# VectorE in program order at the ends of the feed-forwards and through the Fourier mixing, and x += in quarters

## The chip, the cores and the metric

The kernel runs on one core of one Trainium2 chip. The metric is the device time of one execution in microseconds (us). Engines are called as the profile calls them: PE (TensorE, matrix products), DVE (VectorE), ACT (ScalarE), POOL (GpSimd), SP (SyncE, which issues nearly all DMAs).

## The reference, cut to what matters

Two layers work on 256 tokens of 2048 features. Layer 0 mixes by windowed attention and a gated delta rule, layer 1 by a two-dimensional Fourier transform. Each mixing ends in a square projection, and each layer in a feed-forward:

```python
def fourier_mix(h):
    hg = h.astype(jnp.float32).reshape(b, l, FOURIER_GROUPS, FOURIER_GROUP_DIM)
    y = jnp.fft.fft2(hg, axes=(1, 3), norm='ortho').real
...
for layer in range(DEPTH):
    mx = split(silu_c @ w_ada[layer] + b_ada[layer], N_MOD)
    h_x = modulate(rms_norm(x, g_pre_mix[layer]), mx[0], mx[1])
    y_x = attention_deltanet_mixer(h_x, ...)  or  fourier_mix(h_x) @ w_fourier[o]
    x = x + mx[2] * rms_norm(y_x, g_post_mix[layer])
    f_x = swiglu(modulate(rms_norm(x, g_pre_ffn[layer]), mx[3], mx[4]), w_gate, w_up, w_down)
    x = x + mx[5] * rms_norm(f_x, g_post_ffn[layer])
```

So there are four places at which a product y is normalized, scaled and added to x: after w_out and after the feed-forward in layer 0, after w_four (the kernel's name for w_fourier) and after the feed-forward in layer 1. At the first three a norm of the new x follows at once, ahead of the next products.

## The kernel before, in words

**Products.** The 256 tokens are two tiles (t = 0, 1) of 128. A weight tile of 128 x 1024 (512 KB) comes by DMA into `raw` (4 buffers) or `araw` (2 buffers). Each half of it is split into two parts for a product of full precision: ACT writes the high part `whi` (L198), DVE the low part `wlo` (L204), or POOL does for a share of them (`pool_share`). Both have 4 buffers, so splits run two weight tiles ahead of PE. PE does three matmuls for each half and token tile: 12 for a weight tile and both token tiles.

**The four ends** are all `out_proj`. The output has four strips of 512 features. Strips 0 to 2 do both token tiles together. The last strip goes by token tile: all of t = 0, then all of t = 1, with some of the split weights kept (in ZT, T, A, KTOK, VTOK). Here POOL takes a quarter of the low parts. Behind each token tile comes `tail`: `evac_y` (in a feed-forward the sum of two halves, L1143; then ACT squares it, L1145, and DVE multiplies it by the row of gains, L1146), the reciprocal root (L322 to L327), x += in pieces of 1024, 512 and 512 columns (L1169), squares of the new x on ACT (L1172), the second reciprocal root (L1179 on), and a diagonal matrix `St` (L1181). `pre_norm` then makes pieces of the normed x: PE multiplies x by `St`, ACT and DVE scale and shift (L1222), ACT copies the high part, DVE subtracts the low part (L1225), through an `E2` tile. E2 has 3 buffers, of which the matrices of the Fourier transform hold two during the mixing. At the end of the kernel, instead of squares, each x += piece is followed by a DMA to the output.

**The Fourier mixing** calls `over_d` (a product over the features of a group) for 6 groups of t = 0 first, then, group by group, `over_d` of t = 1 and `over_l` (a product over tokens).

**Modulation weights.** `silu(c) @ w_ada` is 320 dot products on DVE (L275, 128 x 1024 each, called ada dots here), each with a 512 KB DMA into `araw`. `every(us)` sets the pace at which the program puts them between other work; `ada_until(m)` puts in all that remain up to modulation m. In `out_proj` that is called behind strip 2. Pieces of pending work (`fin_y`, `tail`) are generators: `add` queues one, each `yield d` puts the rest d us later on a modelled clock of PE, `step` resumes what is due, `drain` finishes it.

**Order.** Outside `in_order(True)` a scheduler sets the order of all engines. Inside, DVE keeps the order in which the program was written, and the scheduler orders the others. Before, `in_order(True)` is switched off ahead of the last strip of every `out_proj`. SP, like every engine, works through its list in order: a DMA into a buffer that is still in use holds up those behind it.

## Time and profile before

| | |
|---|---|
| median of 3 runs | 2500.32 us (2495.74 to 2503.1) |
| the profiled execution | 2498.01 us, its span 2496.2 us (1.8 us lie around it) |
| granted PE clock | 0.978 of full speed, mean over the span |
| PE busy | 2382.9 us, 95% of the span |
| DVE, ACT, POOL busy | 1791.7, 1284.7, 84.7 us |

PE's busy time also counts matmuls that ran at half clock, and a wait of PE is where another engine or a DMA was late. The profile is of one execution, so sums over its rows are to be held against 2498.01 us, and the other runs show how far one execution lies from the next.

### The profile page before, as it was taken

What the parts mean: (1) busy time and instruction counts of PE and PEld (TensorE: products, weight loads), DVE (VectorE), ACT (ScalarE), POOL (GpSimd) and SP (SyncE); (2) the same over time, 40 slices, a digit from 0 to 9 for tenths busy, and PEclk for the clock granted to TensorE, in tenths of its full rate; (3) what the DMA queues carried; (4) which work ended last, traced back from release to release, by engine and by line L of the source; (5) the groups of instructions that cost most, each with busy time, mean ns of one, the idle gap of its engine ahead of it and who ended that gap; (6) DMA issues with size and microseconds to landing.
All of it is one profiled execution on the core that took longest, in us unless ns stands there. A gap on an engine that the chain in (4) does not pass through costs nothing.

```text
span 2496.2 us, 39579 instructions
## 1 busy us (share of the span) xinstructions
PE 2382.9 (95%) x14536; PEld 1982.1 (79%) x14536; DVE 1791.7 (72%) x3379; ACT 1284.7 (51%) x2314; POOL 84.7 (3%) x106
## 2 busy tenths in 40 slices
PE   7999899988999999999999999799999999999997
PEld 6888688966778788888888887777888888888886
DVE  5889788877575787777777787878666666555566
ACT  5347345463755645444454545546554544445455
POOL 1000000000000100000000001002000000000001
PEclk8999999989999999999999999999999999999998
DMA  8885777668256589888888898586576777656665
GB/s 302 289 291 180 230 226 259 210 219 275 69 185 205 177 309 314 311 306 317 318 311 313 309 321 305 206 294 217 189 239 233 234 238 243 192 183 190 189 202 192
DMA packets 218483, 611.04 MB, mean 245 GB/s; under 512 B 68904, under 2 KB 69912, under 8 KB 217520
## 3 DMA queue, kind: packets, MB, share of 16 engines
q1 hardware_dynamic: 168016, 581.59, 68.4%
q10 hardware_dynamic: 46528, 15.21, 2.5%
q0 software_dynamic: 3744, 11.71, 1.4%
q8 instruction: 114, 1.87, 0.3%
q14 instruction: 81, 0.66, 0.1%
HBM read 595.03 MB, written 13.40 MB: 244 GB/s over the span
## 4 chain that ended last, share of the span: by engine, by line
PE 78%; DVE 8%; DMA 7%; ACT 3%; issue 3%; POOL 0%; ACTq 0%; DVEq 0%; POOLq 0%
PE acc L133 68%; PE sm L133 9%; DMA araw<-in_ada_d 3%; DVE wlo L204 2%; DVE araw L275 2%; DVE C L524 1%; DVE S L1169 1%; PE sm L1252 1%; DMA T<-dz 1%; DMA dy<-T 1%; DMA T<-dy 1%; ACT whi L198 1%; DMA araw<-in_w_dn 0%; DMA dz<-Zc 0%; DMA smallr<-in_smallr 0%
## 5 line engine op out<-in xcount | busy, mean ns | idle before, releaser
L198 ACT ACTIVATE whi<-raw 128x512 fp32r<-128x512 f32 (+1 forms) x1324 | 831.1, 630 | 895.7 <-DVE wlo L204 465.5
L204 DVE TENSOR_TENSOR wlo<-raw,whi 128x512 fp32r<-128x512 f32 (+1 forms) x1306 | 893.9, 692 | 482.9 <-ACT whi L198 480.3
L133 PE MATMUL acc<-whi,S 128*128 128x512 f32 x3312 | 1058.6, 397 | 6.6 <-ACT whi L198 5.4
L133 PEld LDWEIGHTS acc<-whi,S 128*128 128x128 f32 x3312 | 626.5, 189 | 142.8 <-ACT whi L198 5.8
L133 PE MATMUL acc<-wlo,S 128*128 128x512 f32 x1656 | 650.6, 393 | 2.0 <-DVE wlo L204 2.0
L275 DVE SCALAR_TENSOR_TENSOR araw<-araw,cb 128x1024 f32<-128x1024 f32 x320 | 389.1, 1218 | 33.8 <-DMA araw<-in_ada_d 33.1
L133 PEld LDWEIGHTS acc<-wlo,S 128*128 128x128 f32 x1656 | 313.6, 189 | 72.5 <-DVE wlo L204 3.4
L133 PE MATMUL acc<-S,whi 128*128 128x256 f32 x1152 | 221.3, 287 | 3.1 <-DVE C L524 3.0
L133 PEld LDWEIGHTS acc<-S,whi 128*128 128x128 f32 x1152 | 184.1, 192 | 4.0 <-issue 3.1
L133 PE MATMUL acc<-S,wlo 128*128 128x256 f32 x576 | 163.3, 284 | 2.0 <-DVE wlo L204 2.0
L133 PE MATMUL acc<-whi,ZT 128*128 128x512 f32 x384 | 122.0, 391 | 0.0
L133 PEld LDWEIGHTS acc<-S,wlo 128*128 128x128 f32 x576 | 110.8, 192 | 2.7 <-DVE wlo L204 2.6
L133 PE MATMUL acc<-whi,KCH 128*128 128x512 f32 x320 | 111.1, 404 | 1.1 <-ACT whi L198 1.1
L133 PE MATMUL acc<-whi,A 128*128 128x512 f32 x312 | 105.5, 393 | 0.0
L133 PE MATMUL acc<-whi,T 128*128 128x512 f32 x296 | 99.5, 392 | 0.0
L133 PE MATMUL acc<-wlo,KCH 128*128 128x512 f32 x192 | 78.7, 410 | 7.0 <-DVE wlo L204 6.8
L133 PEld LDWEIGHTS acc<-whi,ZT 128*128 128x128 f32 x384 | 72.2, 188 | 15.2
L133 PE MATMUL acc<-wlo,ZT 128*128 128x512 f32 x192 | 75.5, 393 | 0.2 <-POOL wlo L204 0.2
L133 PEld LDWEIGHTS acc<-whi,KCH 128*128 128x128 f32 x320 | 62.2, 195 | 15.1 <-ACT whi L198 1.5
L133 PE MATMUL acc<-wlo,T 128*128 128x512 f32 x176 | 68.9, 391 | 0.0
L133 PEld LDWEIGHTS acc<-whi,A 128*128 128x128 f32 x312 | 58.6, 188 | 11.9
L133 PEld LDWEIGHTS acc<-whi,T 128*128 128x128 f32 x296 | 55.6, 188 | 12.2
(442 smaller groups left out, 2638.0 us busy)
## 6 DMA issues: line engine op xcount, KB each, us to landing
raw<-in_w_gu SPq DMA_DIRECT2D x347, 512.0 KB, 4.3
araw<-in_ada_d SPq DMA_DIRECT2D x320, 512.0 KB, 4.8
raw<-in_w_dn SPq DMA_DIRECT2D x179, 512.0 KB, 4.6
raw<-in_w_att SPq DMA_DIRECT2D x40, 512.0 KB, 4.5
raw<-in_w_gdn SPq DMA_DIRECT2D x34, 512.0 KB, 4.6
raw<-in_w_out SPq DMA_DIRECT2D x30, 512.0 KB, 3.5
raw<-in_w_four SPq DMA_DIRECT2D x30, 512.0 KB, 4.3
ZT<-in_ada_s SPq DMA_DIRECT2D x24, 512.0 KB, 4.5
```

Source lines behind the costliest of these rows:

```text
L133: nc.tensor.matmul(out, l, r, start=start, stop=stop)
L198: S.activation(hi[:, :w], raw[:, c:c + w], AF.Copy)
L204: eng.tensor_sub(lo[:, :w], raw[:, c:c + w], hi[:, :w].bitcast(F32))
L275: V.scalar_tensor_tensor(out=junk, in0=w, scalar=1.0, in1=rows, op0=ALU.mult, op1=ALU.mult, accum_out=dst)
L524: V.scalar_tensor_tensor(out=ca[:, :, lo:hi], in0=pv[:, :, lo + o:hi + o], scalar=wconv[:, blk, j:j + 1], in1=ca[:, :, lo:hi], op0=ALU.mul ...
L1169: V.scalar_tensor_tensor(out=x[:, t, sl], in0=y[:, t, sl], scalar=r, in1=x[:, t, sl], op0=ALU.mult, op1=ALU.add)
L1252: nc.tensor.transpose(p[:, i * P:(i + 1) * P], hv[t][:, i * P:(i + 1) * P], ident)
```

## The change

1. `in_order(add_)` stands in `out_proj` where `in_order(False)` stood. `add_` is true for the two feed-forwards' second halves, so DVE keeps the program's order through their last strips and tails. After the first feed-forward that lasts through the norm and the whole Fourier mixing, up to the new `in_order(False)` ahead of w_four. At the ends of w_out and w_four the scheduler orders DVE as before.
2. x += goes in four quarters of 512 columns, with `yield TY` (0.7 us on the modelled clock) ahead of each; the wait of 2.5 us ahead of the second root is gone. Other work of the program falls between the quarters.
3. In the last strip of a feed-forward the sum goes to an E2 tile instead of in place.
4. The output goes by 2 DMAs for t = 0 and 3 for t = 1, in place of 3 and 3.
5. In the mixing `drain("tail1")` finishes the second token tile's x += before the loop over groups, ada dots come at a pace of 2.6 us from there on, pending work is resumed in `over_d` and `over_l`, and the first weights of w_four are fetched at group 7.

```diff
+F9RATE = 2.6
-YSQ = 2.5
+TY = 0.7
...
         if add_:
-            V.tensor_tensor(out=dst, in0=p, in1=dst, op=ALU.add)
-            src = dst
+            src = e2([P, 512]) if n == 3 else dst
+            V.tensor_tensor(out=src, in0=p, in1=dst, op=ALU.add)
...
-            sq = col(3)
-            for h, sl in enumerate((slice(0, 1024), slice(1024, 1536), slice(1536, 2048))):
+            yield TY
+            sq = col(4)
+            for h in range(4):
+                sl = slice(h * 512, h * 512 + 512)
                 V.scalar_tensor_tensor(out=x[:, t, sl], in0=y[:, t, sl], scalar=r, in1=x[:, t, sl],
                                        op0=ALU.mult, op1=ALU.add)
                 if emit is None:
                     S.activation(y[:, t, sl], x[:, t, sl], AF.Square, accum_out=sq[:, h:h + 1])
-                else:
-                    emit(t, sl)
+                elif t == 0 and h % 2:
+                    emit(t, slice(h * 512 - 512, h * 512 + 512))
+                elif t == 1 and h:
+                    emit(t, slice(0, 1024) if h == 1 else sl)
+                yield TY
             if emit is not None:
                 return
-            yield YSQ
...
         every(0)
         ada_until(mods)
-        in_order(False)
+        in_order(add_)
...
     for g in range(FAHEAD):
         over_d(g, 0)
+    drain("tail1")
+    every(F9RATE)
     for g in range(9):
...
+        if g == 7:
+            pool_share[0] = 0.0
+            while len(ahead) < 1 + AHEAD:
+                ahead.append(load_w1(*seq.pop(0)) if isinstance(seq[0], tuple) else load_w1(seq.pop(0)))
     every(FRATE)
-    pool_share[0] = 0.0
     ada_until(7)
+    in_order(False)
     rows = make_row(mc[:, 1, 2], gains[:, 1, 1])
```

Lines shift by 1 to 5: L204 becomes L205, L275 L276, L1143 L1145, L1146 L1147, L1169 L1172, L1181 L1186, L1222 L1227, L1225 L1230. How the orders move is shown at three places; the number at the end of a name tells one tile from another.

**The end of the second feed-forward.** DVE behind t = 0 of the last strip, first before (acc_23836 is the product of t = 0, the next row's `wlo` belong to weights of t = 1):

```order
L204 TENSOR_TENSOR wlo_24044<-raw_24041,whi_24043 128x512
L1146 TENSOR_TENSOR S_1240_8401<-S_1240_8401,OG_23132 128x512
L324 TENSOR_SCALAR col_24026<-ssy_23135,col_24024 128x1
L204 TENSOR_TENSOR wlo_24048<-raw_24041,whi_24047 128x512
L325 RECIPROCAL col_24025<-col_24025 128x1
L326 SCALAR_TENSOR_TENSOR col_24027<-col_24025,col_24026 128x1
L1162 TENSOR_REDUCE col_24159<-ssy_23135 128x1
L327 SCALAR_TENSOR_TENSOR col_24025<-col_24027,col_24025 128x1
L322 TENSOR_SCALAR col_24165<-col_24159 128x1
L204 TENSOR_TENSOR wlo_24060<-araw_24057,whi_24059 128x512
L1169 SCALAR_TENSOR_TENSOR S_1234_8386<-S_1240_8401,col_24025,S_1234_8386 128x1024
L1169 SCALAR_TENSOR_TENSOR S_1234_8386<-S_1240_8401,col_24025,S_1234_8386 128x512 x2
```

and now:

```order
L1145 TENSOR_TENSOR E_5054_24033<-acc_23855,S_1240_8401 128x512
L1147 TENSOR_TENSOR S_1240_8401<-E_5054_24033,OG_23149 128x512
L323 TENSOR_SCALAR col_24044<-col_24028 128x1
L325 TENSOR_SCALAR col_24046<-ssy_23152,col_24044 128x1
L326 RECIPROCAL col_24045<-col_24045 128x1
L327 SCALAR_TENSOR_TENSOR col_24047<-col_24045,col_24046 128x1
L328 SCALAR_TENSOR_TENSOR col_24045<-col_24047,col_24045 128x1
L205 TENSOR_TENSOR wlo_24057<-raw_24054,whi_24056 128x512
L205 TENSOR_TENSOR wlo_24061<-raw_24054,whi_24060 128x512
L1172 SCALAR_TENSOR_TENSOR S_1234_8386<-S_1240_8401,col_24045,S_1234_8386 128x512
L205 TENSOR_TENSOR wlo_24075<-araw_24072,whi_24074 128x512
L1172 SCALAR_TENSOR_TENSOR S_1234_8386<-S_1240_8401,col_24045,S_1234_8386 128x512
```

All three pieces of x += stood between two splits before. Now a split or two stands between every two quarters. The splits that stood between the small instructions of the root are behind them now.

**The start of the Fourier mixing.** DVE behind t = 1 of the first feed-forward's last strip, before (acc products end, pieces L1222 and L1225 of t = 0, ada dots L275):

```order
L1146 TENSOR_TENSOR S_1240_8401<-S_1240_8401,OG_15078 128x512
L324 TENSOR_SCALAR col_16329<-ssy_15081,col_16327 128x1
L325 RECIPROCAL col_16328<-col_16328 128x1
L1225 TENSOR_TENSOR S_3190_16210<-E_3195_16219,S_3189_16209 128x4x128
L326 SCALAR_TENSOR_TENSOR col_16330<-col_16328,col_16329 128x1
L275 SCALAR_TENSOR_TENSOR araw_16785,adaacc_15850<-araw_16785,cb 128x1024
L1222 TENSOR_SCALAR E_3197_16231<-sm_16226,psc_16207,mc 128x128 x2
L143 TENSOR_TENSOR ZT_16212<-sm_16213,ZT_16211 128x258
L143 TENSOR_TENSOR ZT_16212<-sm_16246,ZT_16211 128x258
L1225 TENSOR_TENSOR S_3190_16210<-E_3197_16231,S_3189_16209 128x4x128
L327 SCALAR_TENSOR_TENSOR col_16328<-col_16330,col_16328 128x1
L275 SCALAR_TENSOR_TENSOR araw_16832,adaacc_15850<-araw_16832,cb 128x1024
```

and now:

```order
L1145 TENSOR_TENSOR E_3201_16258<-acc_16036,S_1240_8401 128x512
L1147 TENSOR_TENSOR S_1240_8401<-E_3201_16258,OG_15082 128x512
L144 TENSOR_TENSOR ZT_16221<-sm_16257,ZT_16220 128x258
L1227 TENSOR_SCALAR E_3205_16277<-sm_16272,psc_16216,mc 128x128 x2
L1230 TENSOR_TENSOR S_3191_16219<-E_3205_16277,S_3190_16218 128x4x128
L323 TENSOR_SCALAR col_16284<-col_16247 128x1
L325 TENSOR_SCALAR col_16286<-ssy_15085,col_16284 128x1
L326 RECIPROCAL col_16285<-col_16285 128x1
L327 SCALAR_TENSOR_TENSOR col_16287<-col_16285,col_16286 128x1
L328 SCALAR_TENSOR_TENSOR col_16285<-col_16287,col_16285 128x1
L144 TENSOR_TENSOR ZT_16221<-sm_16271,ZT_16220 128x258
L1172 SCALAR_TENSOR_TENSOR S_1234_8386<-S_1240_8401,col_16285,S_1234_8386 128x512
```

The ada dots are gone from here (the first stands behind `St` of t = 1), the root follows on piece 3, and the quarters of x += stand one by one between the splits of the mixing (L144).

**The change from strip 2 to the last strip of w_four.** DVE before (ZT_17381 is the low part of the last strip's second weight tile, wlo_17396 of its third):

```order
L204 TENSOR_TENSOR wlo_17256<-raw_17249,whi_17255 128x512
L204 TENSOR_TENSOR ZT_17381<-araw_17379,ZT_17381 128x512
L204 TENSOR_TENSOR wlo_17277<-raw_17274,whi_17276 128x512
L204 TENSOR_TENSOR wlo_17281<-raw_17274,whi_17280 128x512
L204 TENSOR_TENSOR wlo_17396<-araw_17393,whi_17395 128x512
L204 TENSOR_TENSOR wlo_17400<-araw_17393,whi_17399 128x512
L204 TENSOR_TENSOR wlo_17415<-raw_17412,whi_17414 128x512
L1146 TENSOR_TENSOR S_1240_8401<-acc_17125,OG_16734 128x512
L1162 TENSOR_REDUCE col_17515<-ssy_16737 128x1
L322 TENSOR_SCALAR col_17529<-col_17515 128x1
```

and now (ZT_17394 belongs to the second weight tile, wlo_17409 to the third):

```order
L205 TENSOR_TENSOR wlo_17327<-raw_17320,whi_17326 128x512
L276 SCALAR_TENSOR_TENSOR araw_17380,adaacc_15854<-araw_17380,cb 128x1024
L276 SCALAR_TENSOR_TENSOR araw_17383,adaacc_15854<-araw_17383,cb 128x1024
L1147 TENSOR_TENSOR S_1240_8401<-acc_17171,OG_16790 128x512
L276 SCALAR_TENSOR_TENSOR araw_17386,adaacc_15854<-araw_17386,cb 128x1024
L1147 TENSOR_TENSOR S_1240_8401<-acc_17172,OG_16790 128x512
L290 TENSOR_REDUCE mc<-adaacc_15854 128x16
L1163 TENSOR_REDUCE col_17528<-ssy_16793 128x1
L291 TENSOR_TENSOR mc<-mc,bada 128x16
L323 TENSOR_SCALAR col_17542<-col_17528 128x1
L1208 SCALAR_TENSOR_TENSOR psc_17658<-mc,gains 128x16
L205 TENSOR_TENSOR ZT_17394<-araw_17392,ZT_17394 128x512
```

SP at the same place, now (araw_17392 and araw_17406 are the second and third weight tiles of the last strip):

```order
L287 DMA araw_17377<-in_ada_d 128x1024
L189 DMA raw_17425<-in_w_four 128x1024
L287 DMA araw_17380<-in_ada_d 128x1024
L189 DMA raw_17444<-in_w_four 128x1024
L287 DMA araw_17383<-in_ada_d 128x1024
L287 DMA araw_17386<-in_ada_d 128x1024
L189 DMA raw_17460<-in_w_four 128x1024
L189 DMA araw_17392<-in_w_four 128x1024
L189 DMA araw_17406<-in_w_four 128x1024
```

Before, the last ada dot stood some 20 rows ahead of this place, among the splits for strip 1. Now 11 of them are in the mixing in place of 20; they go on through strip 2, and the last five stand among the splits at its end; the loads of the last strip's second and third weight tiles take the two `araw` buffers behind the last two dots.

## Rows read from the trace of the kernel before

**Rows 1.** The page's section 1: busy us, share of the span and instructions of each engine.

```profile
PE 2382.9 (95%) x14536; PEld 1982.1 (79%) x14536; DVE 1791.7 (72%) x3379; ACT 1284.7 (51%) x2314; POOL 84.7 (3%) x106
```

**Rows 2.** Windows: stretches of the span, busy us and instructions of each engine.

```profile
core 0: us, PE busy (x) PEld busy (x) DVE busy (x) ACT busy (x) POOL busy (x), PEclk, DMA share, GB/s
806.00:842.00 36.00, 32.06 (x167) 26.08 (x166) 30.24 (x66) 27.10 (x61) 8.46 (x6) 1.00 0.48 158
1463.00:1515.00 52.00, 52.00 (x229) 42.26 (x228) 43.45 (x72) 25.92 (x44) 0.00 (x0) 1.00 0.92 329
...
1560.00:1582.00 22.00, 16.65 (x81) 13.44 (x79) 19.07 (x42) 17.24 (x36) 4.29 (x4) 0.92 0.72 253
1582.00:1602.00 20.00, 11.54 (x70) 10.27 (x71) 17.75 (x42) 10.43 (x26) 0.00 (x0) 0.83 0.46 157
...
1645.00:1702.00 57.00, 56.62 (x239) 46.02 (x240) 42.64 (x69) 29.36 (x52) 1.52 (x1) 0.97 0.81 287
1702.00:1756.00 54.00, 48.06 (x219) 37.42 (x218) 45.34 (x87) 39.97 (x86) 14.05 (x10) 0.94 0.64 213
2466.00:2496.20 30.20, 16.74 (x60) 12.45 (x58) 18.38 (x31) 11.50 (x21) 4.46 (x4) 0.77 0.37 138
```

**Rows 3.** Timeline of PE, five stretches; in brackets the wait ahead and its releaser.

```profile
1566.03 0.50 PE L133 MATMUL acc<-wlo,A 128*128 128x512 f32 x1 [3.11 <-DVE wlo L204]
...
1575.22 1.95 PE L133 MATMUL sm<-St,S 128*128 128x128 f32 x16
...
1594.31 3.78 PE L133 MATMUL sm<-St,S 128*128 128x128 f32 x16 [6.79 <-DVE St L1181]
...
1645.38 0.51 PE L133 MATMUL acc<-wlo,KCH 128*128 128x512 f32 x1 [2.70 <-DVE wlo L204]
...
1740.50 0.73 PE L133 MATMUL acc<-ZT,S 128*128 128x512 f32 x2 [1.69 <-ACT S L1224]
...
2476.43 0.79 PE L133 MATMUL acc<-wlo,KCH 128*128 128x512 f32 x1 [3.05 <-DVE wlo L204]
```

**Rows 4.** Timeline of DVE: four of the eight x += groups, and the last multiply.

```profile
1561.76 3.62 DVE L1169 SCALAR_TENSOR_TENSOR S<-S,col,S 128x1024 f32<-128x1024 f32 x3
...
1735.43 3.65 DVE L1169 SCALAR_TENSOR_TENSOR S<-S,col,S 128x1024 f32<-128x1024 f32 x3
...
2471.12 4.65 DVE L1169 SCALAR_TENSOR_TENSOR S<-S,col,S 128x1024 f32<-128x1024 f32 x3
...
2487.47 0.69 DVE L1146 TENSOR_TENSOR S<-S,OG 128x512 f32<-128x512 f32 x1 [0.79 <-ACT K L1145]
...
2488.85 2.61 DVE L1169 SCALAR_TENSOR_TENSOR S<-S,col,S 128x1024 f32<-128x1024 f32 x3
```

**Rows 5.** Timeline of POOL beside the first and the third of these groups.

```profile
1562.80 1.36 POOL L204 TENSOR_TENSOR wlo<-araw,whi 128x512 fp32r<-128x512 f32 x1 [2.45 <-DMA raw<-in_w_dn]
...
2471.00 1.36 POOL L204 TENSOR_TENSOR wlo<-araw,whi 128x512 fp32r<-128x512 f32 x1 [4.48 <-ACT whi L198]
2473.95 1.27 POOL L204 TENSOR_TENSOR wlo<-raw,whi 128x512 fp32r<-128x512 f32 x1 [1.59 <-ACT whi L198]
```

**Rows 6.** Timeline of DVE at the start of the Fourier mixing.

```profile
1576.27 0.68 DVE L1143 TENSOR_TENSOR S<-acc,S 128x512 f32<-128x512 f32 x1
...
1593.97 0.28 DVE L1181 TENSOR_SCALAR St<-ident,col 128x128 f32<-128x128 f32 x1
```

**Rows 7.** Timeline of DVE at the start of the w_four projection.

```profile
1643.49 1.23 DVE L275 SCALAR_TENSOR_TENSOR araw<-araw,cb 128x1024 f32<-128x1024 f32 x1 [4.43 <-DMA araw<-in_ada_d]
```

**Rows 8.** DMA issues between 1632 and 1702 us: KB each, median us to landing.

```profile
raw<-in_w_four SPq DMA_DIRECT2D x23, 512.0 KB, 4.3
araw<-in_ada_d SPq DMA_DIRECT2D x10, 512.0 KB, 5.1
```

**Rows 9.** Page, section 5: groups by line; busy us, mean ns of one, idle before.

```profile
L198 ACT ACTIVATE whi<-raw 128x512 fp32r<-128x512 f32 (+1 forms) x1324 | 831.1, 630 | 895.7 <-DVE wlo L204 465.5
...
L275 DVE SCALAR_TENSOR_TENSOR araw<-araw,cb 128x1024 f32<-128x1024 f32 x320 | 389.1, 1218 | 33.8 <-DMA araw<-in_ada_d 33.1
```

More of the change, by code (lines that the diff above doesn't have):

```diff
@@ L1172, in tail @@
                     S.activation(y[:, t, sl], x[:, t, sl], AF.Square, accum_out=sq[:, h:h + 1])
-                else:
-                    emit(t, sl)
+                elif t == 0 and h % 2:
[3 more added lines that the diff above has]
+                yield TY
             if emit is not None:
                 return
-            yield YSQ
             s1 = col(1)
-            V.tensor_reduce(out=s1, in_=sq[:, 0:2], op=ALU.add, axis=AX.X)
-            r = rstd_m2(s1, sq[:, 2:3], D)
+            V.tensor_reduce(out=s1, in_=sq[:, 0:3], op=ALU.add, axis=AX.X)
+            r = rstd_m2(s1, sq[:, 3:4], D)
             V.tensor_scalar(dg[:, t], ident, r, -0.5, ALU.mult, ALU.mult)
@@ L1375, in over_d @@
             src = hsl(2 * g + kc, t)
+            step()
             for x_, y_ in three:
@@ L1390, in over_l @@
                         i += 1
+                step()
         yh, yl = yt[g // 2]
@@ L1424, in trunk @@
     drain()
+    in_order(False)
 def consts():
```

## The prediction

> **What bounds the kernel now.** I read the page first, then windows, then PE's timeline wherever a window showed PE short of work. PE is busy for 2382.9 us, 95% of its span of 2496.2 [rows 1], so everything that engine order can give back lies in some 113 us of PE's idle time and in matmuls at half clock. The windows say where. In long products PE has no gap (52.00 of 52 us, 229 matmuls, so 0.227 us for one and 2.7 us for the 12 of a weight tile). It falls short at the places that this change touches: 32.06 of 36 at the end of w_out, 16.65 of 22 in the last strip of the first feed-forward, 11.54 of 20 at the start of the mixing, 48.06 of 54 at the end of w_four, 16.74 of 30.2 at the end of the kernel [rows 2].
>
> The timeline names what was late. In both feed-forwards' last strips PE waits once for a low part: 3.11 and 3.05 us [rows 3]. On DVE the x += group of t = 0 stands ahead of these low parts, for 3.62 and 4.65 us [rows 4]. At the mixing the wait is 6.79 us for `St` [rows 3], which DVE starts at 1593.97, 17.7 us after it took up the last product at 1576.27 [rows 6]. At w_four's start PE waits 2.70 us for a low part [rows 3], and DVE had just started an ada dot for which it had waited 4.43 us, until its DMA landed [rows 7]. The 1.69 us at 1740.50 come right after an x += group of 3.65 us [rows 3, 4].
>
> A wait costs more than itself, since PE then works at half clock for a while: 16 matmuls take 1.95 us at 1575.22, but 3.78 us after the wait for `St` [rows 3]. The windows with such waits have granted clocks of 0.92, 0.83 and 0.77, against 1.00 in the long products [rows 2]; the two levels are 2.4 and 1.2 GHz. I price the stretch behind a wait of about 3 us at 1.5 to 2.5 us.
>
> **The change, part by part.** Plus is time saved.
>
> (a) End of the first feed-forward. The split that PE waited for is now behind one quarter of x += and no longer behind the group. The same 2048 columns take 2.61 us in the last group [rows 4], so a quarter takes 0.65 to 0.75. But the small instructions of the root and the two 0.69 us instructions of `evac_y`, between which splits stood before, now come ahead of the splits in one run, with DVE waiting for ACT's square in it (0.79 us where the last one shows it [rows 4]). I count some 3 us in which no split is made, in place of 3.6 plus those small ones, and more evenly spread after that. Of 3.11 plus 1.5 I take +1.7; bounds 0 (the same wait in another place) and +4.6.
>
> (b) Start of the mixing. 4 ada dots stood in DVE's way to `St`, 1.22 us each [rows 9]; now none do, which alone is +4.9. Against it, program order puts the sum of t = 1 into the one free E2 buffer, behind piece 2 of t = 0 and ahead of piece 3, and the root behind piece 3, which waits for ACT twice. Then come four quarters, each between splits that wait for PE and ACT. Chained by hand with 0.7 us for each large instruction and 2.5 us for a piece through E2, the sum starts 7 us after the last product, the quarters 13, and `St` 20.5 to 22.5; it was 18.8 (1575.22 to 1593.97). I take 2 us later, -2; bounds -5 and +2. The ada dots inside the mixing cost nothing while PE has its products: 11 take 13 us of DVE, where 20 took 24.
>
> (c) Start of w_four. The dots come evenly now and fewer are in flight there, so the wait of 4.43 us for one dot's DMA should not return. 2.70 plus 1.6 at half clock was lost; I take +3, bounds 0 and +4.3.
>
> (d) The change from strip 2 to the last strip of w_four. This is the part that speaks against the change. 20 ada dots now lie behind the mixing in place of 11, and the last five stand at the end of strip 2. They go through two `araw` buffers, so each load starts when the dot before the last is done, and takes 5.1 us [rows 8]. By hand, from the start of strip 2: 12 us until the fifth weight tile's split frees DVE for dot 17374, done at 13.7; so dot 17380 has its data at 18.8; dot 17377 ends at 18.5, so dot 17383 has its data at 23.6 and is done at 24.9. Only then can SP issue araw_17392, the last strip's second weight tile: it lands 4.3 us later [rows 8], and 0.63 us of ACT [rows 9] makes it 29.9. PE needs it at 23.2 (8 weight tiles at 2.72 and half a one). Before, that load was issued some 25 us ahead and PE went through there without a wait: 56.62 of 57 us were busy from 1645 to 1702 [rows 2]. So 6.7 us of waiting and about 1.5 at half clock, less a little that the other engines catch up: -7.5. Bounds: 0, should the scheduler's order on DVE run further ahead of PE than I think and the dots be done in time, and -10.
>
> (e) End of w_four and the norm behind it. Pieces of t = 0 no longer stand behind 3.65 us of x += for t = 1, from which PE's wait of 1.69 us came and a slower stretch behind it (the window's granted clock is 0.94 [rows 2]). `St` of t = 1 comes behind three more splits. +2, bounds 0 and +5. At the end of w_out, of the same form, DVE's order hardly moves: +0.5, bounds 0 and +1.
>
> (f) End of the second feed-forward. As in (a), but the group took 4.65 us, and behind 3.05 us of waiting came 2.4 us of half clock. I take +4, bounds +1 and +5.6. Behind the last product the multiply no longer waits 0.79 us for ACT's square [rows 4], since the sum has a tile of its own; the root still waits for the square, so 0.5. Four quarters in place of three pieces cost 0.1; one DMA less is off the end. +4.4 in all.
>
> Sum: 1.7 - 2 + 3 - 7.5 + 2.5 + 4.4 = **+2.1 us**. The profiled execution (2498.01) would become 2495.9, the median (2500.32), which is 2.3 us higher, 2498.2. I forecast **2497 us**, no change that can be told: a measurement of this kernel shows about 0.3%, or 7.5 us.
>
> **A rule weighed.** The x += group of 3.62 us has one POOL split beside it, that of 4.65 has two [rows 4, 5], and the last one of 2.61 comes when POOL has no split left: one POOL split costs such a group 1.0 us. The Trainium skill, page "SBUF — State Buffer", section "Who interferes with whom", says that a DVE instruction with two inputs in SBUF and a GpSimd instruction that reads SBUF exclude each other for a whole instruction, whichever starts first. The trace agrees in kind, at 1.0 us for each, where the whole POOL instruction is 1.27 to 1.36 us [rows 5]. By that rule quarters that stand alone could each meet a POOL split, where a group met one or two. In rows of this case: 4 quarters with a POOL split each would lose 4 us in place of 1 or 2, at two feed-forward ends, so the sum would fall by 4 to 5 us, to -3. I hold that against (a) and (f): POOL makes only a quarter of the low parts there, and a POOL split that meets no x += meets a low part on DVE. I give it 1 in 10, inside the forecast's range.
>
> **Rivals.**
>
> *The dots are done in time.* If (d) does not happen, the rest stands: +9.6, 2488 to 2491 us. For it: the loads overlap, and DVE's dots in strips 0 and 1 ran without PE waiting before. Against it: two buffers and a landing of 5.1 us set a pace that no order changes, and SP stands still for the loads behind. 0.28.
>
> *`St` comes much later.* Slower: in program order a single late split holds up every quarter behind it. If `St` of t = 1 starts 27 us after the last product rather than 21, (b) is -8 with the half clock behind it, and the sum about -5; with (d) at its lower end, -8. 2503 to 2508 us. It decides from 25 us on. For it: PE already falls to 11.54 of 20 us here [rows 2], and each piece crosses PE, ACT and DVE. Against it: four ada dots have left. 0.15.
>
> *The change does little.* The waits for low parts return at the next split, since DVE has the same work in the same strip (18.38 us busy of the last 30.2 [rows 2]) and ACT's halves come no sooner: (a), (c) and (f) at a third, (d) halved. 2499 to 2502. 0.07.
>
> **How the numbers follow.** Forecast 0.5, rivals 0.28, 0.15, 0.07. The forecast's own range is 2492 to 2503. To leave out 2 in 10 the range takes in most of the first two rivals: 2487 to 2506. Faster by over 0.3% (below 2492.8): nearly all of the first rival and a little of the forecast, 0.30. Slower (above 2507.8): the second rival with (d) at its lower end, and some of the forecast where bounds meet, 0.15. Same: 0.55.
>
> **What would show it.** (a), (f): PE's waits for a low part in the last strips below 2 us, with no x += longer than 1.3 us on DVE. (b): `St` 20.5 to 22.5 us after the last product. (c): no wait of PE above 1 us in the first strip of w_four. (d): one wait of PE of 4 to 8 us behind the first weight tile of w_four's last strip, ended by ACT's high part of a tile in `araw`, whose DMA was issued late. The forecast is wrong if that wait is missing, or if a new one of over 3 us stands inside the mixing, where PE had none.

## The result and the profile after

The changed kernel takes 2511.32 us (median of 6 runs, 2508.89 to 2515.91), the kernel before 2497.44 us beside it (6 runs): ratio 1.0055, 95% interval 1.0039 to 1.0072. It is slower, by 14 us. The profiled execution took 2514.42 us, with a span of 2512.6; before it was 2498.01 and 2496.2.

Windows of the changed kernel, columns as in [rows 2]. The clock of its times is its own, so the same work stands some us later:

```profile
806.00:842.00 36.00, 33.24 (x174) 27.67 (x173) 31.92 (x71) 29.48 (x68) 9.55 (x6) 1.00 0.51 161
...
1560.00:1582.00 22.00, 17.16 (x83) 12.05 (x81) 16.08 (x32) 16.11 (x35) 5.78 (x4) 1.00 0.73 236
1582.00:1602.00 20.00, 10.02 (x48) 8.31 (x48) 12.27 (x34) 9.43 (x26) 0.00 (x0) 0.66 0.00 1
...
1645.00:1702.00 57.00, 52.12 (x216) 41.35 (x216) 40.32 (x67) 24.68 (x44) 0.00 (x0) 0.97 0.88 306
1702.00:1756.00 54.00, 45.40 (x193) 33.89 (x193) 43.44 (x84) 36.09 (x78) 12.12 (x10) 0.94 0.75 258
...
2466.00:2512.00 46.00, 32.20 (x130) 23.12 (x128) 33.56 (x53) 24.35 (x44) 11.10 (x8) 0.94 0.57 192
```

The stretch from 1582 to 1602 has fallen to 10.02 us of PE work with a granted clock of 0.66, and those from 1645 and 1702 have lost 4.5 and 2.7 us. PE's timeline names the waits:

```profile
1562.20 0.50 PE L134 MATMUL acc<-wlo,A 128*128 128x512 f32 x1 [1.05 <-DVE wlo L205]
...
1597.61 3.79 PE L134 MATMUL sm<-St,S 128*128 128x128 f32 x16 [6.42 <-DVE St L1186]
...
1652.83 0.61 PE L134 MATMUL acc<-wlo,KCH 128*128 128x512 f32 x1 [3.69 <-DVE wlo L205]
...
1710.00 0.40 PE L134 MATMUL acc<-ZT,A 128*128 128x512 f32 x1
1717.10 1.52 PE L134 MATMUL acc<-ZT,T 128*128 128x512 f32 x2 [6.71 <-ACT ZT L199]
...
2475.53 0.50 PE L134 MATMUL acc<-wlo,KCH 128*128 128x512 f32 x1 [1.69 <-DVE wlo L205]
...
2489.55 0.50 PE L134 MATMUL acc<-wlo,A 128*128 128x512 f32 x1 [1.03 <-DVE wlo L205]
```

Of the two single waits of 3.11 and 3.05 us [rows 3] pieces are left, the longest 1.05 us at the first end and 1.69 us at the second, below 2 us as forecast. But at the second end there are seven of them, 4.7 us in all. The wait for `St` is 6.42 us, hardly shorter than before (6.79). Two others are longer: 3.69 us in w_four's first strip (2.70 before), and 6.71 us behind the first weight tile of w_four's last strip, which was not there before.

To set stages side by side I read from the timelines when PE reaches nine places, and took the eight intervals between them. So the time up to the norm behind w_out drops out, which differed by up to 12 us between profiles. The change touches only its end, w_out's first x +=, and from the small matmul that spreads w_out's gains to that norm it is 77.5 us in both kernels. The places, before and after: first matmul with `St` behind w_out (819.19, 820.12); the small matmul that spreads the gains in the first feed-forward (1454.82, 1453.79); last product of its last strip (1574.98, 1575.58); first matmul with the second `St` of the mixing (1594.31, 1597.61); the small matmul behind the mixing (1631.19, 1634.87); first matmul of w_four's last strip (1702.19, 1708.84), of its third weight tile (1704.94, 1720.14); the small matmul in the second feed-forward (2367.60, 2384.17); end of the last product (2485.96, 2503.03). Each column is the interval up to a place, in us more (+) or less than before. A row is one profile of each kernel, and the last column is the sum. The columns of the feed-forwards begin where the gains are spread, so each holds all four strips of that projection; "its last strip" holds only the first two weight tiles of that strip:

```
               w_out  ffn 1   to St  mixing  w_four  its last  rest,   ffn 2    sum
               end    strip 3        rest    0 to 2  strip     norm    strip 3
after          -2.0   +1.6    +2.7   +0.4    +3.0    +8.6      +1.4    +0.5    +16.1
after_again    -1.9   +1.3    +2.4   +1.6    +0.2    +8.1      +0.6    +0.5    +12.7
no_araw        -2.0   +2.3    +2.7   +0.4    +2.6     0.0      +3.9    -0.1     +9.8
dots_pace      -1.1   +3.5    +2.7   +0.4    +1.7    +1.6      -0.2    +0.5     +8.9
dots_early     -1.9   +2.6    +5.2   +3.0     0.0     0.0      -0.4    +0.5     +9.0
dots_both      -2.0   +3.3    +4.9   +2.8    +2.2    +1.6      +1.7    +0.5    +15.0
no_dots        -1.9   +3.4    +2.7   +1.6    -4.6     0.0      -0.4    +0.5     +1.2
mix_free       -2.0   -1.2    +7.5   +1.2    +2.8     0.0      -0.2    +0.5     +8.6
strip_free     -2.0   -1.8    +3.1   +1.6    +1.6    +8.9      -0.3    -0.1    +11.1
inplace_1      -2.0   +1.6    +2.7   +0.4    +1.2    +8.3      +1.9    +0.5    +14.5
tail_first     -1.1   +4.1    -0.4 (both)    +0.9    +9.8      +2.5    +0.5    +16.2
old_tail        0.0   +2.1    +1.9   +1.7    +0.8    +7.9      -0.5    +2.4    +16.3
own_n2         -1.9   +1.3    +3.0   +1.7    +1.6    +8.2      +2.6    +0.4    +16.7
ffn1_free      -1.9   +2.9    +2.7   +1.6    +1.4    +7.7      +2.4    -3.0    +13.6
three_ends     -2.0   -0.2     0.0    0.0    -0.5     0.0      -0.4    -2.0     -5.0
```

Two profiles of the same kernel (after, after_again) agree within 0.8 us in six columns, but differ by 2.8 us in w_four's strips 0 to 2 and by 1.2 us in the rest of the mixing. The experiments whose edits lie elsewhere show a wider spread: +1.3 to +3.5 in the first feed-forward, -0.3 to +2.6 behind the first tiles of w_four's last strip. A column is worth no more than that; steady are `St` at +2.4 to +2.7 and the second feed-forward at -0.1 to +0.5. Behind the last product 9.6 us are left, 10.2 before. The same kernel a second time, beside three experiments:

> The changed kernel once more, unaltered, beside the next three on one chip. All theories: 2508 to 2512 us where before stands at 2497, ratio 1.004 to 1.007.

It measured 2506.25 us, ratio 1.0051 (1.0033 to 1.0069).

### The profile page after: what moved, and what is told of

It reads as the page before. It is cut to its first block, busy times and chain, and to the rows that moved or that the text cites. A ratio compares the mean times of both kernels' runs of the same rounds, so it can differ in the third digit from the quotient of the medians.

```text
span 2512.6 us, 39611 instructions
## 1 busy us (share of the span) xinstructions
PE 2387.6 (95%) x14536; PEld 1980.1 (79%) x14536; DVE 1792.7 (71%) x3387; ACT 1287.8 (51%) x2326; POOL 86.3 (3%) x106
## 4 chain that ended last, share of the span: by engine, by line
PE 74%; DVE 9%; DMA 9%; issue 5%; ACT 3%; ACTq 0%; SPq 0%; POOL 0%; DVEq 0%; POOLq 0%
PE acc L134 65%; PE sm L134 8%; DMA araw<-in_ada_d 4%; DVE wlo L205 2%; DVE araw L276 2%; DMA T<-dz 1%; PE sm L1257 1%; DMA dy<-T 1%; DMA OG<-in_ada_s 1%; DVE C L525 1%; ACT whi L199 1%; DMA T<-dy 1%; DVE S L1172 1%; DMA dz<-Zc 0%; DVE E L276 0%
## 5 line engine op out<-in xcount | busy, mean ns | idle before, releaser
L205 DVE TENSOR_TENSOR wlo<-raw,whi 128x512 fp32r<-128x512 f32 (+1 forms) x1306 | 895.4, 695 | 459.6 <-ACT whi L199 457.5
L276 DVE SCALAR_TENSOR_TENSOR araw<-araw,cb 128x1024 f32<-128x1024 f32 x320 | 389.9, 1220 | 50.4 <-DMA araw<-in_ada_d 50.0
```

The costliest lines, as they stand in the source:

```text
L205: eng.tensor_sub(lo[:, :w], raw[:, c:c + w], hi[:, :w].bitcast(F32))
L276: V.scalar_tensor_tensor(out=junk, in0=w, scalar=1.0, in1=rows, op0=ALU.mult, op1=ALU.mult, accum_out=dst)
```

## The longest wait: five dots, two buffers

The rows of the changed kernel at the change to w_four's last strip, on SP (DMA issues):

```profile
1706.17 2.08 SPq L287 DMA_DIRECT2D araw<-in_ada_d  x2
1708.35 0.37 SPq L189 DMA_DIRECT2D raw<-in_w_four  x1
1711.98 2.07 SPq L189 DMA_DIRECT2D araw<-in_w_four  x2
```

on DVE:

```profile
1704.92 1.22 DVE L276 SCALAR_TENSOR_TENSOR araw<-araw,cb 128x1024 f32<-128x1024 f32 x1
...
1706.66 1.22 DVE L276 SCALAR_TENSOR_TENSOR araw<-araw,cb 128x1024 f32<-128x1024 f32 x1
...
1710.72 1.22 DVE L276 SCALAR_TENSOR_TENSOR araw<-araw,cb 128x1024 f32<-128x1024 f32 x1 [2.83 <-DMA araw<-in_ada_d]
...
1712.48 1.21 DVE L276 SCALAR_TENSOR_TENSOR araw<-araw,cb 128x1024 f32<-128x1024 f32 x1
...
1717.08 0.69 DVE L205 TENSOR_TENSOR ZT<-araw,ZT 128x512 fp32r<-128x512 f32 x1 [2.26 <-ACT ZT L199]
```

and on ACT:

```profile
1716.41 1.15 ACT L199 ACTIVATE ZT<-araw 128x512 fp32r<-128x512 f32 x2 [6.69 <-DMA araw<-in_w_four]
```

The dot at 1710.72 had waited 2.83 us for its load, issued at 1706.17 as soon as the dot two ahead had ended. It ends at 1711.88, and 0.1 us later SP issues the last strip's second weight tile, into the buffer just freed. That lands 4.4 us later at 1716.41, where ACT had waited 6.69 us, and PE goes on at 1717.10. So buffer, load, dot and load again stand in a chain, as forecast. If this is the cause, other buffers or fewer dots behind strip 2 take the wait away. Rivals were DVE's own time for the dots, and a general shortage of DMA.

**Other buffers (no_araw).**

```diff
-        raw = T([P, 1024], "araw", 2) if pace[1] and not pace[0] and nload[0] % 5 > 2 else T([P, 1024], "raw", 4)
+        raw = T([P, 1024], "araw", 2) if pace[1] and not pace[0] and nload[0] % 5 > 2 and not inmix[0] else T([P, 1024], "raw", 4)
```

(`inmix` is true from the start of w_four to the second feed-forward.)

> The changed kernel, but the weight tiles of w_four's last strip never use the two buffers of the ada dots; they take the four raw buffers. Same number of dots in every stage. Theory: the wait of 6 to 7 us behind the first weight tile of that strip is the load of the second tile, which can't be issued before the dot in its buffer is done; with other buffers the load is issued in time, the wait is at most 1.5 us, and the time falls by 6 to 8 us against the changed kernel, ratio 0.998 to 1.002. Rival: DVE's own work on five dots and their late data hold up the splits in DVE's queue whatever the buffer; then PE still waits 3 us or more there.

PE's timeline at the second weight tile shows no wait:

```profile
1700.42 0.39 PE L134 MATMUL acc<-ZT,A 128*128 128x512 f32 x1
1700.65 0.62 PE L134 MATMUL acc<-ZT,T 128*128 128x512 f32 x2
```

The time is 2501.52 us, ratio 1.0040 (1.0023 to 1.0057). The wait is gone with all dots in place, so the theory stands and DVE's time for the dots was not it. But by the table's sum only 3 to 6 of the 8 us came back: with four buffers for all weight tiles of the strip PE waits more often later, five times for 0.2 to 1.0 us between 1703 and 1711 us. That column is +3.9, where the runs that leave it alone have -0.3 to +2.6. So the `araw` buffers probably had a use there.

**Fewer dots behind strip 2 (dots_pace).**

```diff
-FRATE = 5.0
+FRATE = 2.8
```

> The changed kernel with one number changed: in the w_four projection the program puts in an ada dot every 2.8 us of its modelled clock in place of 5.0, so that none remain to be put in together behind strip 2. DVE keeps about the same number of dots in the projection, but only two stand behind the last splits of strip 2 and not five. Theory: the wait of 6.7 us at the last strip comes from the loads of its second and third weight tiles, queued behind the last five dots; it falls below 2 us, and the time falls by 6 to 9 us against the changed kernel, ratio to before 0.999 to 1.003. Rival: DMA is short in the whole projection, because nine more loads lie there; then the wait only moves to other strips and the time stays within 3 us of the changed kernel.

The wait fell to 0.6 us, and the column from +8.6 to +1.6. The profile was 2500.4 us long, yet the runs say 2506.06 us, ratio 1.0053 (1.0034 to 1.0071), where the sum of the row would be 1.0036. The profiled execution was the fastest of its six, and the median is that of the changed kernel, as the rival said. The mechanism is shown by the profile, the gain is not shown by the runs.

**Dots ahead of `St` (dots_early).**

```diff
+    every(F9RATE)
     for g in range(FAHEAD):
         over_d(g, 0)
     drain("tail1")
-    every(F9RATE)
```

> The changed kernel with one line moved: the pace of 2.6 us for ada dots begins ahead of the pieces of the first token tile in the mixing and not behind them, so three more dots come ahead of St of the second tile, in program order on DVE. Theory: the 20 us without DMA shrink and three fewer dots are left to w_four, so the wait at its last strip is 3 to 4 us and not 6.7; St comes up to 2 us later; the time falls by 2 to 5 us against the changed kernel. Rival: DVE's order ahead of St is so tight that each dot delays St by its whole 1.3 us and PE goes on at half clock longer; then the time stays the same or grows.

Three dots moved, and the whole 8.6 us of the last strip went, and the 3 us ahead of it too. But `St` came 2.5 us later than in the changed kernel, most of the 3.7 us that three dots take, and the rest of the mixing lost 1.4 to 2.6 us more. 2503.92 us, ratio 1.0043 (1.0028 to 1.0058). Both expectations were half right.

**Both (dots_both).** The two edits above together.

> The changed kernel with both changes to the dots' pace: it begins ahead of the first norm pieces, and in w_four it is 2.8 us. So no dot is left to be put in behind strip 2. Theory: the wait at w_four's last strip is gone (below 1 us), and what remains of the loss against before is the first feed-forward's end (1.5 us), the mixing's start (2.5 to 5 us) and the second feed-forward's end (0.5 us), less 2 us won at w_out: ratio 1.001 to 1.003. Rival: the dots' loads then compete with the weights in all strips and the loss in strips 0 to 2 grows to 4 us or more; ratio above 1.004.

2513.52 us, ratio 1.0077 (1.0060 to 1.0094): the worst. The last strip did lose its wait, but `St` waits longest of all, as PE shows:

```profile
1602.70 3.57 PE L134 MATMUL sm<-St,S 128*128 128x128 f32 x15 [9.08 <-DVE St L1186]
```

and w_four's strips lose 2.2 us again, with more dots in them. So theory and rival were both too simple: more dots cost ahead of `St`, and they cost in w_four. The stretch behind `St` was not tried: from 1602 to 1632 us PE of the changed kernel is busy for 29.29 of 30 us with nine dots in it, DVE for 22.57, and no experiment changed the pace there.

**No dots in w_four (no_dots).** From the seventh row of that modulation on the loads and dots are skipped and the sums set to zero:

```diff
-                        raw = T([P, 1024], "araw", 2)
-                        nc.sync.dma_start(raw, a["ada_d"][n, h])
-                        ada_dot(raw, cb[:, h], ac[:, k, h:h + 1], raw)
+                        if 134 <= n < 144:
+                            if n == 134 and h == 0:
+                                V.memset(ac[:, 6:], 0.0)
+                        else:
+                            raw = T([P, 1024], "araw", 2)
+                            nc.sync.dma_start(raw, a["ada_d"][n, h])
+                            ada_dot(raw, cb[:, h], ac[:, k, h:h + 1], raw)
```

> The changed kernel without the last 20 of the 32 ada dots of one modulation (their part of the sum is left out, set to zero), that is without any dot or dot's load in the w_four projection. The 11 dots in the mixing stay. Theory: dots in w_four cost 3 us in strips 0 to 2 (a wait for a dot's load) and 8 us at the last strip; without them both go, and the time is 9 to 12 us below the changed kernel, ratio to before 0.999 to 1.002, with 4 to 5 us of loss left at the first feed-forward's end and the start of the mixing, less 2 us won at w_out. Rival: w_four's first wait comes of the weights' own loads or of the row that is spread over the partitions there, not of the dots; then a wait of 2 to 3 us stays in strip 0.

2494.69 us, ratio 0.9999 (0.9985 to 1.0012), the table's two w_four columns at -4.6 and 0.0, and no wait of PE in w_four's strips 0 to 2. So the waits there hung on dots, by the same place also the 2.70 us of before with its half clock [rows 3]: by these two columns dots cost 4.6 us in the kernel before and 13 to 16 in the changed one. The rival falls.

Why are there more of them there? In the changed kernel no dot can run ahead of the second tile's `St`, since DVE's program order puts the first behind it. The loads of two dots fill their buffers, and SP stands at the third. DMA between 1580 and 1602 us (busy tenths and GB/s in 40 slices of 0.55 us), and SP's row:

```profile
DMA  0000000100000000000000000000000000000000
GB/s 22 0 0 0 0 0 0 30 0 0 0 0 0 0 0 0 0 0 0 0 0 0 0 0 0 0 0 0 0 0 0 0 0 0 0 0 0 0 0 0
```

```profile
1575.74 58.21 SPq L287 DMA_DIRECT2D araw<-in_ada_d  x11
```

11 issues take from 1575.74 to 1633.95; the first is at 1575.74, the second only at 1607.38, behind the first dot. Before, DMA moved 157 GB/s from 1582 to 1602 [rows 2]; now almost nothing moves for 20 us. The nine dots that w_four takes over are 4.7 MB of loads, 19 us at the mean rate of the kernel's page (243 GB/s).

## The first feed-forward's end and the mixing

DVE of the changed kernel at the start of the mixing:

```profile
1577.43 0.73 DVE L1227 TENSOR_SCALAR E<-sm,psc,mc 128x128 f32<-128x128 f32 x2 [1.64 <-ACT E L1225]
1578.92 0.69 DVE L1230 TENSOR_TENSOR S<-E,S 128x512 fp32r<-128x512 f32 x1 [0.76 <-ACT S L1229]
1580.55 0.73 DVE L1227 TENSOR_SCALAR E<-sm,psc,mc 128x128 f32<-128x128 f32 x2 [0.94 <-ACT E L1225]
...
1583.05 0.68 DVE L1145 TENSOR_TENSOR E<-acc,S 128x512 f32<-128x512 f32 x1
...
1585.58 0.73 DVE L1227 TENSOR_SCALAR E<-sm,psc,mc 128x128 f32<-128x128 f32 x2 [0.78 <-ACT E L1225]
...
1588.53 0.16 DVE L326 RECIPROCAL col<-col 128x1 f32<-128x1 f32 x1 [0.46 <-ACT col L324]
...
1597.27 0.29 DVE L1186 TENSOR_SCALAR St<-ident,col 128x128 f32<-128x128 f32 x1
```

DVE is not busy here: 12.27 of 20 us in the window. PE's waits for pieces ahead of `St` are seven with 5.2 us in all; before they were three with 3.2 us. A piece takes 3.1 us (1577.43 to 1580.55), with 0.76 to 1.64 us of waiting for ACT between its steps; the sum of the second tile (L1145), ready from 1576, comes at 1583.05 behind piece 2; the root at 1588.53 behind piece 3; `St` at 1597.27, 21.7 us after PE's last product.

**In the scheduler's order (mix_free).**

```diff
-        in_order(add_)
+        in_order(add_ and emit is not None)
```

> The changed kernel, but DVE's order in the first feed-forward's last strip and through the Fourier mixing is the scheduler's, as before (program order only at the end of the second feed-forward). Theory: the loss comes from program order in the mixing, which keeps the ada dots behind St of the second token tile, lets DMA stand still for 20 us and leaves 9 more dots to the w_four projection. Then the dots are back in the mixing, the wait of 6.7 us at w_four's last strip and the one of 3.7 us in its first strip go, and the time is 2495 to 2500 us, ratio to before 0.998 to 1.001. Rival: the quarters and the sum in an E2 tile cost as much by themselves, whatever the order; then it stays above 2505 us, ratio above 1.003.

2499.77 us, ratio 1.0031 (1.0016 to 1.0046): the ratio lies just above the rival's bound, the time is in the theory's range. The wait at w_four's last strip went, as the theory has it, and the feed-forward won 1.2 us over before. A wait of 3.89 us in w_four's first strip stayed, against the theory. Here DMA did not stand still (174 GB/s from 1582 to 1602 us), and between 1632 and 1702 us only 8 dots' loads were issued, where before had 10 [rows 8] and the changed kernel 18. So that wait needs dots, as no_dots shows, but neither the standstill nor more of them. And `St` came still later, which no theory had:

```profile
1597.62 3.78 PE L134 MATMUL sm<-St,S 128*128 128x128 f32 x16 [5.93 <-DVE St L1186]
...
1651.88 0.79 PE L134 MATMUL acc<-wlo,KCH 128*128 128x512 f32 x1 [3.89 <-DVE wlo L205]
```

`St` is used 26.9 us after the last product (1570.75). Quarters, the pace of the dots and the late `drain` lose 7.5 us here in the scheduler's order, more than in program order (2.7). So program order is a help at this place, and the rest of the edit delays `St` where the scheduler has the order. Which part of it does so no run tells apart.

**Program order from the mixing on (strip_free).** As mix_free, and `in_order(True)` ahead of the mixing's first `over_d`.

> The changed kernel, but the first feed-forward's last strip is in the scheduler's order, and program order begins behind it, at the first norm piece of the mixing. Theory: program order loses 1.5 us in that last strip, because DVE waits for ScalarE's squares and root with splits queued behind; that comes back, and the rest of the loss (mixing, w_four) stays: 1 to 3 us below the changed kernel, its last product 1.5 us earlier in the profile. Rival: that loss comes of the quarters in that strip; then the last product comes no earlier.

The last product came 3.4 us earlier by the table (-1.8 in place of +1.6; the profiles in program order have +1.3 to +3.5, and mix_free, in the scheduler's order there too, -1.2). So program order is what loses in that strip; the quarters by themselves win there. 2506.12 us, ratio 1.0043 (1.0030 to 1.0056).

**The sum in place (inplace_1).**

```diff
-            src = e2([P, 512]) if n == 3 else dst
+            src = e2([P, 512]) if n == 3 and own[0] else dst
```

(`own` is true in the second feed-forward.)

> The changed kernel, but the sum of the first feed-forward's last strip is made in place, as before, and not in an E2 tile; the second feed-forward keeps its E2 tile. Theory: at the start of the mixing only one E2 buffer is free, each norm piece holds it for 3.1 us, and the sum of the second token tile takes a turn in that line. Without it St of the second tile comes 2 to 3 us earlier after the last product, and the time falls by 2 to 4 us against the changed kernel. Rival: the line is DVE's program order and not the buffer, and in place the multiply waits 0.79 us for the square; then St comes no earlier and the time stays.

Nothing: `St` at +2.7 as in the changed kernel, 2506.42 us, ratio 1.0051 (1.0032 to 1.0070). My theory of the single E2 buffer falls; the multiply then waits for the square (0.87 us) in place of it.

**The tail first (tail_first).**

```diff
+    drain("tail1")
     for g in range(FAHEAD):
         over_d(g, 0)
-    drain("tail1")
```

> The changed kernel with one line moved: the x += of the second token tile is finished ahead of the first norm pieces of the mixing, in program order, and not behind them. Theory: St of the second tile is late because program order puts the sum behind piece 2, the root behind piece 3 and the quarters around piece 4, and each piece takes 3.1 us through ScalarE and VectorE in turn. With the tail first St comes about 10 us after the last product and not 21, the first pieces come 7 to 8 us later, and the wait for St goes; the start of the mixing gains 1 to 3 us in all. Rival: PE has nothing else to do ahead of the first piece, so the wait only moves there and half clock follows it; then the mixing ends later than in the changed kernel.

The wait for `St` is gone, and PE waits for the first pieces:

```profile
1582.09 3.03 PE L134 MATMUL sm<-C,S 128*128 128x258 f32 x12 [7.92 <-ACT S L1229]
...
1594.92 0.76 PE L134 MATMUL sm<-C,S 128*128 128x258 f32 x4 [2.32 <-ACT S L1229]
```

From the last product to the end of the mixing it is 55.8 us against 59.3 and 60.2 in the two profiles of the changed kernel and 56.2 before. But that last product came 2.4 us later, in a column that other runs move by up to 1.9 us without an edit there, and the runs show no gain: 2505.99 us, ratio 1.0051 (1.0035 to 1.0067). What decides the start of the mixing, other than that pieces and tail pass through ACT and DVE in turn, stays open.

## The ends of the feed-forwards

DVE of the changed kernel at the end of the second feed-forward, and ACT in its root:

```profile
2469.50 1.18 DVE L1147 TENSOR_TENSOR S<-S,OG 128x512 f32<-128x512 f32 x1 [0.79 <-ACT K L1146]
...
2484.18 0.69 DVE L1145 TENSOR_TENSOR E<-acc,S 128x512 f32<-128x512 f32 x1 [0.38 <-PE acc L134]
2484.90 0.69 DVE L1147 TENSOR_TENSOR S<-E,OG 128x512 f32<-128x512 f32 x1
...
2486.14 0.21 DVE L325 TENSOR_SCALAR col<-ssy,col 128x1 f32<-128x1 f32 x1 [0.48 <-ACT K L1146]
2488.27 0.16 DVE L326 RECIPROCAL col<-col 128x1 f32<-128x1 f32 x1 [1.92 <-ACT col L324]
...
2488.80 2.38 DVE L205 TENSOR_TENSOR wlo<-raw,whi 128x512 fp32r<-128x512 f32 x2
2491.11 0.74 DVE L1172 SCALAR_TENSOR_TENSOR S<-S,col,S 128x512 f32<-128x512 f32 x1
...
2495.51 1.77 DVE L1172 SCALAR_TENSOR_TENSOR S<-S,col,S 128x512 f32<-128x512 f32 x1
```

```profile
2486.65 1.28 ACT L324 ACT_TABLE_LOAD   x1
```

From 2483.66 to 2488.80 DVE makes no split. 0.48 and 1.92 us of it are waits for ACT, which makes a split of its own and then loads a table for the root (1.28 us). Before, three splits stood in these gaps. At the first feed-forward's end the stretch without a split is 4.4 us (1557.06 to 1561.45), with the same wait of 1.92 us. Ahead of that, each multiply of strip 2 waits 0.79 us for ACT's square with splits behind it: program order now covers that too, but own_n2 below shows that it costs nothing that the table can tell.

**The second feed-forward in the scheduler's order (ffn1_free).**

```diff
-        in_order(add_)
+        in_order(add_ and emit is None)
```

> The changed kernel, but DVE's order at the end of the second feed-forward is the scheduler's, as before. Theory: program order at that end gives and takes alike (PE waited 3.05 us and ran at half clock before, now it waits 4.7 us in seven pieces), so the time stays within 2 us of the changed kernel, ratio to before 1.004 to 1.006. Rival: program order there costs by itself, since DVE waits for ScalarE's squares and for its root with splits queued behind, and quarters in the scheduler's order would be better than both; then it gains 4 us or more against the changed kernel, ratio below 1.004.

The table's column of that end goes from +0.5 to -3.0, 3.5 us, nearly what the rival called for. The runs (2508.35 us, ratio 1.0058, 1.0040 to 1.0076) show nothing of it: by the ratio set ahead the theory stands. I take the rival as borne out by the profile alone, since that column is steady, and three_ends repeats it below.

**Strip 2 with a tile of its own (own_n2).** `n >= 2` in place of `n == 3` in `evac_y`.

> The changed kernel, but strip 2 of the feed-forwards also makes its sum in an E2 tile. In program order the multiplies of strip 2 wait 0.79 us each for ScalarE's square, with splits behind them, and PE waits 1.7 us for a low part right after it. Theory: that wait falls below 1 us at both feed-forwards' ends, and each gains 0.5 to 1.5 us; the time falls by 1 to 3 us against the changed kernel, too little to be told by the runs, but seen in the two profiles. Rival: what holds the splits there is the length of DVE's queue; then the wait of 1.7 us stays.

The multiplies no longer wait, but DVE's next split then waits 1.50 us for ACT's high part, and PE's wait went only from 1.69 to 1.53 us at the second end. The column did not move (+0.4), 2510.38 us, ratio 1.0071 (1.0056 to 1.0086). The theory falls.

**The old tail (old_tail).** Three pieces in a row, sum in place, `YSQ`, in the changed kernel's order.

> The changed kernel with the tail of before: x += in three pieces in a row, the sum in place, the wait of 2.5 us ahead of the second root; program order and dots as in the changed kernel. Theory: the quarters are not what costs, and the bunch of dots in w_four stays, so the wait of 6 to 7 us at w_four's last strip stays; but at the last strips the three pieces in a row stand ahead of the splits again and PE waits over 2.5 us in one piece, and at w_out and w_four 2 us more are lost. Time 2510 to 2520 us, ratio 1.005 to 1.010. Rival: the quarters cost more than the order; then it falls to 2500 to 2505 us, ratio below 1.003.

2509.87 us, ratio 1.0067 (1.0052 to 1.0081), at the lower end of the theory's range. The 2 us won at w_out are gone, the second end is 1.9 us worse, and single waits of 4.00 and 5.00 us stand at the two ends. So the quarters win there, and what loses is the order and the dots.

**What the experiments pointed to (three_ends).** The kernel before, with the new tail at w_out, at w_four and at the second feed-forward's end, in the scheduler's order everywhere; the first feed-forward's end and the mixing untouched.

> The kernel before, with the quarters of x += at w_out, at w_four and at the end of the second feed-forward (there with the sum in an E2 tile and the output in five DMAs), everything in the scheduler's order; the first feed-forward's end and the mixing stay as before. Theory: the profile of the changed kernel shows 2.0 us won at w_out, and the run with the second feed-forward in the scheduler's order 3.0 us there against before; w_four's end is worth nothing. So it wins 3 to 6 us against before, ratio 0.9976 to 0.9988. Rival: these gains depend on where the scheduler happens to put the pieces; then it stands at 1.000.

2488.81 us (12 runs), ratio 0.9984 (0.9972 to 0.9997): faster than both, by little against the kernel before. Its waits at the last end are two short ones, in place of 3.05 us [rows 3]:

```profile
2467.95 0.51 PE L135 MATMUL acc<-wlo,KCH 128*128 128x512 f32 x1 [0.85 <-DVE wlo L206]
...
2469.64 0.60 PE L135 MATMUL acc<-wlo,KCH 128*128 128x512 f32 x1 [0.72 <-DVE wlo L206]
```

## Why the prediction was wrong, by its own steps

(d) was right: a wait ended by ACT's high part of a tile in `araw`, 6.71 us where 6.7 was worked out, 8.1 to 8.6 us in all for the forecast 7.5. That the first figure fits so closely is luck: in the seven other profiles that have this wait it is 5.83 to 7.09 us. The rival that had the dots done in time is refuted. `St` began 21.7 us after the last product, so the second rival (from 25 us on) did not come either; its sums, -5 and -8, come to -3.9 and -6.4 by its own terms. In the third the waits were to return at the next split; they did so only as short pieces.

(c) failed: +3 was forecast, -3.0 and -0.2 came. The step that failed is that fewer dots are in flight at w_four's start, so that the wait of 4.43 us for one dot's load should not return. 18 dots' loads were issued between 1632 and 1702 us, 10 before [rows 8], and the same wait returned, with 4.84 us for a dot's load in place of 4.43 [rows 7], and 4.20 in the second profile:

```profile
1644.80 0.08 DVE L276 DVE_READ_ACCUMULATOR araw<-araw,cb 128x1 f32 x1
1650.93 1.23 DVE L276 SCALAR_TENSOR_TENSOR araw<-araw,cb 128x1024 f32<-128x1024 f32 x1 [4.84 <-DMA araw<-in_ada_d]
...
1652.08 1.29 DVE L205 TENSOR_TENSOR wlo<-raw,whi 128x512 fp32r<-128x512 f32 x2
```

I had read the order lists for DVE and not asked what SP can issue while DVE holds both buffers. But the number of dots is not the whole of it: mix_free, with 8 such loads and DMA moving ahead of w_four, has the wait too. Why a dot's load comes late just there stays open; only the run without dots there has no such wait.

(a) and (f) failed in the same step: 3 us without a split were counted, 4.4 and 5.1 came, because I left out ACT's table load and its split ahead of the root, which the rows of before hide behind the splits that stood in the gaps. The quarter in place of the group did what was said (waits below 2 us), but +1.7 and +4.4 became -1.6 and about +0.2 (-0.5 up to the last product, +0.7 behind it). In the scheduler's order the same quarters win 1.2 to 1.8 at the first end and 2.0 to 3.0 at the second, so it is the order that loses. That the stretch without splits is how it does so is read from the rows and not tested by itself.

(b) had the sign and nearly the size (`St` 21.7 us after the last product, forecast 20.5 to 22.5; -2 forecast, -3.1 in the profile up to the mixing's end and -4.0 in the second), but the E2 buffer, one of its reasons, was wrong. (e) was 1.5 us too low at w_out and some 3 too high at w_four: +2.5 was forecast in all, +0.6 and +1.3 came. At w_four the wait of 1.69 us went as forecast, but two waits for `St` came that before didn't have, 1.27 and 2.34 us (1.25 and 2.98 in the second profile). The rule weighed (the Trainium skill, page "SBUF — State Buffer", section "Who interferes with whom") cost nothing new. One quarter of four met a POOL split at each feed-forward's end, and took 1.77 us in place of 0.74 (the row at 2495.51 above), 1.0 us as a group did before; so the sign "no x += longer than 1.3 us" failed.

The largest misses, 3 to 6 us for (c), 4 for (f), 3 for (a) and 3 for w_four's end in (e), all go one way and came to more than the range held, since I set each as if independent of the others. For (a) and (f) the cause is the same; that one stands behind all of them is not shown.

## What to carry to other kernels

When an engine's queue is put into program order, look at every instruction in it that waits for another engine or a DMA, and at the queue that fills its buffers: an order that holds a consumer back also holds back the loads, and their work comes back in a later stage. Background work that is taken out of one stage turns up in another; find out which stage has room before moving it. Finer pieces and a fixed order are two changes; at the feed-forwards' ends the pieces win and the order loses, and only separate runs told them apart.

## What I had not expected of the hardware

DMA at 0 to 1 GB/s for 20 us in a kernel that moves 242 GB/s on average, because one queue stood at one wait. PE's clock did what the rows of before had shown: from 1582 to 1602 us PE was busy for 10.02 of 20 us and a mean of 0.66 of full speed was granted, and 16 matmuls that took 1.95 us at 2.4 GHz [rows 3] took 3.79 at 1.2 after 6.42 us of waiting.
